# Gated MLP with split weights: low parts two at a time from a ring of five places, token sums in another rhythm, two early down passes, returns in pieces

## The chip, the cores and the metric

The kernel runs on one core of a Trainium2 chip. Its time is the device time of the program in microseconds (us); the median of several runs counts, and lower is better.

The core's engines work side by side and meet through semaphores: TensorE (PE) multiplies matrices, VectorE (DVE) and ScalarE (ACT) do elementwise work, GpSimd (POOL) has little to do here, and SyncE (SP) issues the DMA transfers. Each engine takes its instructions in the order in which the program lists them.

## The reference, cut to what matters

A decoder trunk of two layers on 256 tokens of width 2048, all in float32. Layer 0 mixes tokens by a block sparse attention (MoBA), layer 1 by a latent attention (MLA), and both are followed by a gated MLP of inner width 5632:

```python
def conv_glu_ffn(h, w_gate, w_up, conv_w, conv_b, w_down):
    g = h @ w_gate
    g = lax.conv_general_dilated(g, conv_w[:, None, :], ..., feature_group_count=g.shape[-1]) + conv_b
    return (jax.nn.silu(g) * (h @ w_up)) @ w_down

for i in range(DEPTH):                       # DEPTH = 2
    h = rms_norm(x, attn_norm[i])
    x = x + mixer(h)                         # MoBA, then MLA
    h = rms_norm(x, ffn_norm[i])
    x = x + conv_glu_ffn(h, ffn_w_gate[i], ffn_w_up[i], ffn_conv_w[i], ffn_conv_b[i], ffn_w_down[i])
```

The change is in the MLPs and in how weights are split for them.

## The kernel before, in words

**Split weights.** Weights come from HBM as float32 in units of 128x1024 (`raw`, 512 KB, six units ahead); a unit is two pieces of 512 columns. TensorE works with rounded numbers, so each piece is split: ACT casts it to a high part (`whi`, line 183), DVE subtracts that from the piece, which gives the low part (`wlo`, line 184). The tokens are split likewise. TensorE then makes three products of a piece: high by high, high by low tokens, low by high tokens (lines 402 to 404, twelve matmuls of 128x256 for a plain piece). The low part is read by the third matmul of a piece first, at line 404.

**The order.** The program is a list of quanta, one per piece, and TensorE goes through them. `ws.split(q + 4)` is called at quantum q, so a piece is split four pieces ahead; `at(q, f)` hangs other work of ACT, DVE and SP on a quantum. High and low parts come from two pools of five tiles, so piece i takes the place of piece i - 5.

**The MLP.** Its 600 pieces a layer are 432 plain ones (gate, up and down projections) and 168 block products. For six groups of four tiles of 128 inner columns, the gate projection is made by a scheme with fewer products: seven products in place of eight, from sums of weights and sums of tokens. A group is 28 products (4 quarters `kq` of the width, seven products each), each six matmuls (lines 1181 to 1183). Three products of a quarter read weights as loaded (`xroom`), four read sums of weights that DVE makes (`weight_sum`, line 1159). Products stand between plain pieces, one or two plain ones for each, by `BLOCK_EVERY`. The matmuls of a group end in transposed form; `mixed` and `cross` (lines 1198 on) add them up in `a_mix`, 14 quanta later DVE's stream transposes (line 516) write the result into `xroom`, four transfers carry it to DRAM (`there<-xroom`), one brings it back. The sum for the next group overwrites the room of the transposes.

**The token sums.** At the start of an MLP, for each quarter, ACT scales four tiles of tokens (`tokens`, line 1072) into `done`, a part of `a_mix`; DVE makes four sums (`token_sum`, line 1088), and these are split in two halves (`token_high`, line 1097; `token_low`, line 1101, 128x512 each). Quarters follow each other at 8 quanta.

**Room.** The tokens `xT` go to DRAM during the MLP (`kept`), and their room holds block weights, weight sums and transposes (`xroom`). Early on, one down pass multiplies the first 16 tiles of inner columns (`DOWN_FIRST` = 4 quarters), so that their room (`a_one`) can be used again; its 16 partial results per layer go to DRAM through ACT copies (`keep_down`, line 1108, `part<-y`, two `y` buffers). Behind the last group, `load_down` fetches them in one transfer (`a_back<-part`, 2048 KB), `leave_room` fetches `xT` in four, two quanta apart, and DVE scales and adds them (`down_scaled`, line 1118, and `down_added`).

Behind that, a pass of plain down pieces ends the layer.

Of the kernel before, what the change touches and what calls it, by code (L numbers as in the profile page):

```python
# [17 lines left out]
P = 128  # L18
S = 256
# [24 lines left out]
AHEAD_PIECES = 4  # L44

# [3 lines left out]
ROOM = 64  # L49
# [13 lines left out]
A_ONE, A_TWO = 4 * DOWN_FIRST, 12  # L63
# [24 lines left out]
class Inner:  # L88


    def __init__(self, pool):
        self.pool, self.tiles = pool, {}
        written = [j for kind, *what in gate_up_order() if kind == "plain" for j in what[:1] if what[1:] == [1, 3]]
        later = [j for j in written if j >= A_ONE]
        homes = ("one", range(A_ONE)), ("two", later[:A_TWO]), ("three", later[A_TWO:])
        self.home = {j: (name, i) for name, js in homes for i, j in enumerate(js)}
        self.size = {name: len(js) for name, js in homes}
        assert self.size["three"] <= A_ONE
        for name in ("one", "two"):
            self.tile(name)  # L100
# [4 lines left out]
    def tile(self, name):  # L105
        if name not in self.tiles:
            n, tag = (A_ONE, "a_one") if name != "two" else (self.size[name], None)
            self.tiles[name] = self.words(name, n, F32R, tag).rearrange("p (j s) -> p j s", s=2 * S)
        return self.tiles[name]
# [7 lines left out]
class Stream:  # L117
# [3 lines left out]
    def __init__(self, nc, raw_pool, part_pool, units, starts, pieces):  # L121
        self.starts = starts
# [4 lines left out]
        self.loaded = self.split_to = 0  # L127

# [35 lines left out]
    def split(self, upto):  # L164
        while self.split_to < min(upto, len(self.pieces)):
            i = self.split_to
            u, j, n = self.pieces[i]
            if u is None:
                b, c = BY_BLOCK
                w = j()  # L170
            else:
                self.load(u + AHEAD_UNITS)
                w = self.raw[u][:, j * n : (j + 1) * n]
                b, c = self.starts(u, j)
            hi = self.part_pool.tile([P, 512 + ROOM], F32R, name="whi")[:, b : b + max(n, 512)]
            lo = self.part_pool.tile([P, 512 + ROOM], F32R, name="wlo")[:, c : c + max(n, 512)]
            hi_, lo_ = hi[:, :n], lo[:, :n]
            if len(w.shape) == 4:
                hi_, lo_ = (x.rearrange("p (i j f) -> p i j f", i=2, j=2) for x in (hi_, lo_))
            if i == 0:  # L180
                self.nc.vector.tensor_copy(hi_, w)
            else:
                self.nc.scalar.copy(hi_, w)  # L183
            self.nc.vector.tensor_tensor(lo_, w, hi_.bitcast(F32), op=ALU.subtract)  # L184
            self.parts[i] = (hi, lo, n)
            self.split_to += 1
            for f, args in self.after.pop(i, ()):
                f(*args)

# [5 lines left out]
def trunk(ctx: ExitStack, tc: tile.TileContext, a, out):  # L195
# [4 lines left out]
    part_pool = ctx.enter_context(tc.tile_pool(name="parts", bufs=AHEAD_PIECES + 1))  # L200
# [25 lines left out]
    block_pieces = {}  # L226

    def gate_up_units(layer):
# [12 lines left out]
        for kind, *what in tokens:  # L241
            if kind == "block":
                block_pieces[(layer, *what)] = len(pieces)
                pieces.append((None, lambda layer=layer, what=what: blocks[layer].source(*what), 512))
            elif kind == "down":
                if at_ % 2 == 0:
# [6 lines left out]
                    downs_unit = len(units) - 1  # L253
                pieces.append((downs_unit, at_ % 2, 512))
                at_ += 1
            else:
                j, up, kq = what
                if kq % 2 == 0:
                    units.append(per[(2 * j + up) * 2 + kq // 2])
                    plain_unit = len(units) - 1  # L260
                pieces.append((plain_unit, kq % 2, 512))
        return pieces

# [24 lines left out]
    ws = Stream(nc, raw_pool, part_pool, units, starts, pieces_of(units))  # L288
# [764 lines left out]
    class Blocks:  # L1053
# [7 lines left out]
        def open(self):  # L1061
# [4 lines left out]
            self.done = mix[:, : 4 * S]  # L1066
# [13 lines left out]
        def token_sum(self, step):  # L1080
            y = self.done.rearrange("p (i e t s) -> p e t i s", i=2, e=2, t=NT)
            a11, a12, a21, a22 = y[:, 0, 0], y[:, 1, 0], y[:, 0, 1], y[:, 1, 1]
            x0, x1 = (self.mix[:, 4 + i].rearrange("p (i s) -> p i s", i=2) for i in range(2))
            out, x, y, op = (
                (x0, a21, a22, ALU.subtract), (x1, a11, a21, ALU.subtract),
                (x1, x0, a11, ALU.subtract), (x0, x1, a12, ALU.add),
# [3 lines left out]
        def token_parts(self, kq, c):  # L1090
            src = self.mix[:, 4:6].rearrange("p c (i s) -> p c i s", i=2)
            hi, lo = (self.parts[:, c : c + 2, 2 * kq : 2 * kq + 2, h] for h in range(2))
            return src, hi, lo

        def token_high(self, kq, c):
            src, hi, _ = self.token_parts(kq, c)
            nc.scalar.copy(hi, src)

        def token_low(self, kq, c):
            src, hi, lo = self.token_parts(kq, c)  # L1100
# [3 lines left out]
        def keep_down(self, state, j):  # L1104
            if j == 0:
                self.part = dram.tile([P, KD, S], F32, name="part")
            y = ffn["pool"].tile([P, S], F32, name="y")
            nc.scalar.copy(y, state["acc"][:, :S])
            nc.sync.dma_start(self.part[:, j], y)

        def load_down(self):
            self.back = ffn["a"].words("back", 8, F32, "a_sums").rearrange("p (j s) -> p j s", s=S)
            nc.sync.dma_start(self.back, self.part)
# [10 lines left out]
        def take_room(self):  # L1124
            room = keep.tile([P, KD * S], F32, name="xroom", tag="xT")
            self.rawq = [room[:, i * 1024 : (i + 1) * 1024] for i in range(2)]
            self.wsum = [room[:, (4 + i) * 512 : (5 + i) * 512] for i in range(4)]
            self.turn = room[:, 6 * 512 :]
# [18 lines left out]
        def total(self, i):  # L1147
            return self.wsum[i].rearrange("p (i j f) -> p i j f", i=2, j=2)

# [128 lines left out]
    def plan_gate(f, q, behind):  # L1278
# [3 lines left out]
        f.ready = behind(q, 9)  # L1282
# [8 lines left out]
    def plan_ffn(layer, norm, next_norm):  # L1291
# [17 lines left out]
        for kind, *what in tokens:  # L1309
# [12 lines left out]
            if kind == "down":  # L1322
                j, kq = what
                opens = kq in (0, DOWN_FIRST)
# [3 lines left out]
                end = (DOWN_FIRST if kq < DOWN_FIRST else NF // 4) - 1  # L1328
                q = add(lambda t_hi, t_lo, n, st=st, kq=kq, opens=opens, end=end: feat_major(
                    st, lambda: ffn["a"], 4 * kq, 4 * end + 3, opens, t_hi, t_lo, n))  # L1330
                if kq == DOWN_FIRST and j == 0:
                    q_down = q
                if kq == DOWN_FIRST - 1:
                    at(behind(q, 2), block.keep_down, st, j)
# [386 lines left out]
    ws.split(1)  # L1721
    for f, args in side.pop(-1):
        f(*args)
    for q, (f, args) in enumerate(quanta):
        for g, gargs in ahead.pop(q, []):
            g(*gargs)
        ws.split(q + min(1 + q // 6, AHEAD_PIECES))
# [10 lines left out]
def gate_up_order():  # L1738

    def full(j):  # L1740
        return [("plain", j, up, kq) for up in range(2) for kq in range(4)]

    def up(j):
        return [("plain", j, 1, kq) for kq in range(4)]
# [4 lines left out]
    def down(j):  # L1749
        return [("down", j, kq) for kq in range(DOWN_FIRST)]  # L1750

    inside = [j for js in BLOCK_GROUPS for j in js]
    fulls = [j for j in range(NF) if j not in inside]
    downs, missing = list(range(KD)), set(range(A_ONE))
    waiting, order, now = [], [], []
    n, ups, most, ready = 0, 0, 2, None

    def plain(k):
        nonlocal now, n, ups, ready
        for _ in range(k):  # L1760
            if not now:
                begun = ready is not None and ready <= n and downs
                if not (waiting or fulls or begun):
                    return
                if waiting and (not (fulls or begun) or (waiting[0][0] <= n and ups < most)):
                    now, ups = up(waiting.pop(0)[1]), ups + 1
                elif begun:
                    now, ups = down(downs.pop(0)), 0
                else:
                    now, ups = full(fulls.pop(0)), 0  # L1770
            order.append(now.pop(0))
            n += 1
            if order[-1][0] == "plain" and order[-1][2:] == (1, 3) and order[-1][1] in missing:
                missing.remove(order[-1][1])
                if not missing:
                    ready = n + DOWN_WAIT

    plain(BLOCK_LEAD)
    for g, js in enumerate(BLOCK_GROUPS):
        for i, one in enumerate(group(g)):  # L1780
            order.append(one)
            plain(BLOCK_EVERY[i % len(BLOCK_EVERY)])
        waiting += [(n + BLOCK_BACK, j) for j in js]
        most = 2 if g + 1 < len(BLOCK_GROUPS) else 4
        plain(BLOCK_GAP)
    plain(8 * NF)
    assert not (downs or fulls or waiting)
    return order + [("down", j, kq) for j in range(KD) for kq in range(DOWN_FIRST, NF // 4)]
# [109 lines left out]
```

## Time and profile before

| | |
|---|---|
| median of 3 runs | 2047.77 us (2047.41 to 2047.81) |
| profiled execution | 2048.13 us, of which the span of the profile is 2045.9 us |
| granted TensorE clock | 1.00 |
| busy share: PE, PEld, DVE, ACT, POOL | 100%, 96%, 81%, 63%, 2% |
| HBM read, written | 411.16 MB, 26.35 MB (214 GB/s) |
| mixed part of the MLP, layer 0 and layer 1 | 382 to 880 us, 1341 to 1840 us |
| last down pass, layer 0 and layer 1 | 880 to 1085 us, 1841 to 2040 us |

How the rows of the profile are read: a group of instructions has its line, engine, operation, output <- inputs by their names in the program, the shape and the count; then, behind a bar, busy us in all and mean ns of one; then the idle time of the engine right before them, with what ended most of it. `L184 DVE ... wlo<-raw,whi` are the low parts of plain pieces, `wlo<-xroom,whi` those of block products. In a timeline a row is start us, duration us, engine, line, operation; idle time before it stands in brackets. In the chain of waits a row is start, duration, engine, tile and line, and a chain runs back from the last instruction over what released each step.

### The profile page before, as it was taken

The page shows a single profiled execution, that of the slowest core. Times are in us where ns is not written, and L with a number is a line of the kernel's source. Part 1 is how long each engine was busy: PE and PEld are TensorE (multiplying, and loading weights), DVE is VectorE, ACT ScalarE, POOL GpSimd, SP SyncE. Part 2 cuts the span into 40 slices and gives each one's busy share as a digit, 9 for nine tenths or more (in the row PEclk, how much of TensorE's full clock was granted, in tenths as well). Part 3 has the DMA queues.
Part 4 walks back from the last instruction along what each step waited for, and adds up shares of the span by engine and source line. Part 5 has one row for each costly group of instructions (what it writes and reads, how often), then busy time and mean ns, then how long its engine had stood idle before and what let it go on. Part 6 is the DMA issues. An engine that isn't in the chain of part 4 may idle for free.

```text
span 2045.9 us, 43563 instructions
## 1 busy us (share of the span) xinstructions
PE 2037.8 (100%) x16300; PEld 1970.4 (96%) x16300; DVE 1660.1 (81%) x3211; ACT 1290.9 (63%) x2474; POOL 48.7 (2%) x38
## 2 busy tenths in 40 slices
PE   9999999999999999999999999999999999999999
PEld 7888899999999999999999889999999999999999
DVE  7877777788998888888666998778889888898655
ACT  6656666666666666655556786666666666666443
POOL 0010000000000000000000110000000000000000
PEclk9999999999999999999999999999999999999999
DMA  7777776676766776676655646567666767758664
GB/s 274 235 250 223 226 231 210 211 233 203 225 218 207 237 239 189 223 267 208 199 196 159 210 152 183 189 214 234 207 214 217 227 217 227 225 186 301 202 211 129
DMA packets 162531, 440.35 MB, mean 215 GB/s; under 512 B 18816, under 2 KB 42880, under 8 KB 162064
## 3 DMA queue, kind: packets, MB, share of 16 engines
q1 hardware_dynamic: 162000, 437.21, 66.6%
q8 instruction: 127, 2.08, 0.4%
q14 instruction: 84, 0.69, 0.1%
q10 hardware_dynamic: 288, 0.33, 0.1%
q0 software_dynamic: 32, 0.04, 0.0%
HBM read 411.16 MB, written 26.35 MB: 214 GB/s over the span
## 4 chain that ended last, share of the span: by engine, by line
PE 97%; DVE 2%; ACT 0%; DMA 0%; issue 0%; SPq 0%; DVEq 0%; ACTq 0%
PE acc L404 23%; PE acc L403 22%; PE acc L402 22%; PE acc L376 16%; PE tp L1183 2%; PE tp L1181 2%; PE tp L1182 2%; PE sc L1183 2%; PE sc L1182 2%; PE sc L1181 2%; DVE wlo L184 1%; PE sc L657 0%; PE sc L656 0%; PE sc L655 0%; PE sc L758 0%; DMA xT<-in_xT 0%
## 5 line engine op out<-in xcount | busy, mean ns | idle before, releaser
L183 ACT CAST whi<-raw 128x512 fp32r<-128x512 f32 (+1 forms) x1271 | 775.6, 621 | 437.4 <-PE acc L403 223.4
L184 DVE TENSOR_TENSOR wlo<-raw,whi 128x512 fp32r<-128x512 f32 (+1 forms) x1272 | 861.1, 689 | 199.0 <-ACT whi L183 170.2
L404 PE MATMUL acc<-h,wlo 128*128 128x256 f32 x2112 | 585.3, 277 | 0.5 <-DVE wlo L184 0.5
L402 PE MATMUL acc<-h,whi 128*128 128x256 f32 x2112 | 585.1, 277 | 0.0
L403 PE MATMUL acc<-h,whi 128*128 128x256 f32 x2112 | 585.0, 277 | 0.0
L404 PEld LDWEIGHTS acc<-h,wlo 128*128 128x128 f32 x2112 | 396.5, 188 | 1.5 <-DVE wlo L184 1.4
L403 PEld LDWEIGHTS acc<-h,whi 128*128 128x128 f32 x2112 | 396.5, 188 | 0.0
L402 PEld LDWEIGHTS acc<-h,whi 128*128 128x128 f32 x2112 | 396.5, 188 | 0.0
L183 ACT CAST whi<-xroom 128x512 fp32r<-128x512 f32 x336 | 208.9, 622 | 102.6 <-PE acc L403 76.6
L376 PE MATMUL acc<-whi,h 128*128 128x512 f32 (+1 forms) x896 | 265.7, 377 | 0.9 <-ACT h L424 0.9
L184 DVE TENSOR_TENSOR wlo<-xroom,whi 128x512 fp32r<-128x512 f32 x336 | 231.1, 688 | 18.9 <-ACT whi L183 9.2
L376 PEld LDWEIGHTS acc<-whi,h 128*128 128x128 f32 x896 | 164.8, 188 | 31.1 <-ACT h L424 1.4
L376 PE MATMUL acc<-wlo,h 128*128 128x512 f32 (+1 forms) x448 | 168.8, 377 | 0.3 <-DVE wlo L184 0.2
L402 PE MATMUL acc<-oT,whi 128*128 128x256 f32 x512 | 142.8, 279 | 0.0
L403 PE MATMUL acc<-a_one,whi 128*128 128x256 f32 x512 | 142.0, 277 | 0.0
L404 PE MATMUL acc<-a_one,wlo 128*128 128x256 f32 x512 | 142.0, 277 | 0.0
L402 PE MATMUL acc<-a_one,whi 128*128 128x256 f32 x512 | 141.9, 277 | 0.0
L404 PE MATMUL acc<-oT,wlo 128*128 128x256 f32 x512 | 141.9, 277 | 0.0
L403 PE MATMUL acc<-oT,whi 128*128 128x256 f32 x512 | 141.8, 277 | 0.0
L402 PE MATMUL acc<-a_three,whi 128*128 128x256 f32 x512 | 141.3, 276 | 0.0
L403 PE MATMUL acc<-a_three,whi 128*128 128x256 f32 x512 | 141.3, 276 | 0.0
L404 PE MATMUL acc<-a_three,wlo 128*128 128x256 f32 x512 | 141.3, 276 | 0.0
(256 smaller groups left out, 3997.8 us busy)
## 6 DMA issues: line engine op xcount, KB each, us to landing
raw<-in_ffn_gu SPq DMA_DIRECT2D x256, 512.0 KB, 4.8
raw<-in_ffn_down SPq DMA_DIRECT2D x144, 512.0 KB, 4.8
xroom<-in_ffn_gu SPq DMA_DIRECT2D x192, 256.0 KB, 4.6
raw<-in_moba_wk SPq DMA_DIRECT2D x32, 512.0 KB, 5.8
raw<-in_moba_wv SPq DMA_DIRECT2D x32, 512.0 KB, 5.0
raw<-in_moba_wo SPq DMA_DIRECT2D x32, 512.0 KB, 4.8
raw<-in_ffn_down SPq DMA_DIRECT2D x64, 256.0 KB, 4.3
raw<-in_mla_wo SPq DMA_DIRECT2D x32, 512.0 KB, 3.8
```

The costliest lines, as they stand in the source:

```text
L183: self.nc.scalar.copy(hi_, w)
L184: self.nc.vector.tensor_tensor(lo_, w, hi_.bitcast(F32), op=ALU.subtract)
L376: mm(state["acc"][t][:, :n], src[:, kt, c : c + P], (t_lo if part == 1 else t_hi)[:, :n], start=kt == 0 and part == 0, stop=kt == k_last a ...
L402: mm(o, w_hi, src[:, kt, :S], start=first and k == 0, stop=False, skip_group_check=True)
L403: mm(o, w_hi, src[:, kt, S:], start=False, stop=False, skip_group_check=True)
L404: mm(o, w_lo, src[:, kt, :S], start=False, stop=kt == k_last, skip_group_check=True)
L1181: mm(o, x[:, 0], w_hi, start=opens and i == 0, stop=False, skip_group_check=True)
L1182: mm(o, x[:, 1], w_hi, start=False, stop=False, skip_group_check=True)
L1183: mm(o, x[:, 0], w_lo, start=False, stop=last and i == 1, skip_group_check=True)
```

## The change

- **Ring.** `whi` and `wlo` become one tile each with five places (`SLOTS`), and a piece takes the place that was used longest ago. In the MLPs, two pieces get one subtraction of 128x2x512 for both low parts, if the ring has two places: the two pieces of a unit, and the weight sums of products 3 and 4, and of 5 and 6. The casts stay one per piece. As built, 432 pairs are so joined and 728 low parts of 512 stay single.
- **Token sums.** Four tokens come within two quanta, the four sums within two, and one `token_high` and one `token_low` take all 1024 columns. `done` is a tile of its own.
- **Down passes.** Two early passes (quarters 0 and 1, quarters 2 and 3) stand in place of one, so 32 partial results a layer go out, in two arrays. The first group has tiles 8 to 11, and groups have 36 plain pieces each.
- **Returns.** `xT<-kept` and `a_back<-part` are asked for in four steps, ten quanta apart, `a_back` in pieces of 512 KB; DVE adds the two partial results (`down_summed`).

```diff
@@ Stream
+        self.high, self.low = (
+            part_pool.tile([P, SLOTS * SLOT], F32R, name=name).rearrange("p (k c) -> p k c", c=SLOT)
+            for name in ("whi", "wlo")
+        )
...
+    def split_these(self, i, now):
...
+        mate, both = self.mates.get(i, (None, None))
+        if mate is not None:
+            held = sum(k >= now for k in self.last_use)
+            wanted = sum(k != mate and k not in self.parts for k in range(i + 1, now + AHEAD_PIECES))
+            if held + 2 + wanted > SLOTS:
+                mate = None
+        these = [i] if mate is None else [i, mate]
+        slots = sorted(sorted(range(SLOTS), key=lambda k: self.last_use[k])[: len(these)])
...
+            two = slice(slots[0], slots[1] + 1, slots[1] - slots[0])
+            hi, lo, src = self.high[:, two, b : b + n], self.low[:, two, c : c + n], both()
+        self.nc.vector.tensor_tensor(lo, src, hi.bitcast(F32), op=ALU.subtract)
@@ constants
-BLOCK_EVERY = 2, 1, 1, 1, 2, 1, 1
-BLOCK_GROUPS = tuple(tuple(range(4 * g, 4 * g + 4)) for g in (0, 6, 7, 8, 9, 10))
-DOWN_FIRST, DOWN_WAIT = 4, 6
+BLOCK_PLAIN = (36,) * 6
+BLOCK_GROUPS = tuple(tuple(range(4 * g, 4 * g + 4)) for g in (2, 6, 7, 8, 9, 10))
+DOWN_PASSES, DOWN_WAIT = (2, 4, NF // 4), 6
@@ plan_ffn
             for k in range(4):
-                at(q + k, block.tokens, 4 * kq + k)
-            at(q + 3, block.keep_tokens, kq)
-            for step in range(2):
-                for half in range(2):
-                    at(q + 4 + 3 * step + half, block.token_sum, 2 * step + half)
-                at(q + 6 + 3 * step, block.token_high, kq, 2 * step)
-                at(q + 7 + 3 * step, block.token_low, kq, 2 * step)
+                at(q + k // 2, block.tokens, 4 * kq + k)
+                at(q + 3 + k // 2, block.token_sum, k)
+            at(q + 2, block.keep_tokens, kq)
+            at(q + 6, block.token_high, kq)
+            at(q + 8, block.token_low, kq)
...
         q = last_block + 9
-        at(q, block.load_down)
         for kq in range(4):
-            at(q + 1 + 2 * kq, block.leave_room, kq)
-        for j in range(0, KD, 2):
-            at(q_down - 12 + 2 * j, block.down_scaled, j)
-            at(q_down - 10 + 2 * j, block.down_added, j)
+            at(q + 1 + 10 * kq, block.leave_room, kq)
+            at(q + 5 + 10 * kq, block.load_down, kq)
+            for j in (4 * kq, 4 * kq + 2):
+                k = q + 17 + 10 * kq + 2 * (j % 4)
+                at(k, block.down_summed, j)
+                at(k + 1, block.down_scaled, j)
+                at(k + 2, block.down_added, j)
```

Three places show what stands in a row on an engine (line, operation, output <- inputs, shape; the lines of the changed program are others: 229 is the low part, 569 the transposes, 1226 the weight sum, 1141 and 1154 the token sums and their low parts). First DVE behind the fifth group of layer 0, before:

```order
L1159 TENSOR_TENSOR xroom<-xroom 128x512
L516 STREAM_TRANSPOSE xroom<-a_mix 128x4x4x32 x2
L184 TENSOR_TENSOR wlo<-raw,whi 128x512
L184 TENSOR_TENSOR wlo<-xroom,whi 128x512
L1159 TENSOR_TENSOR xroom<-xroom 128x512
L1269 TENSOR_TENSOR c<-c,acc 128x256
L184 TENSOR_TENSOR wlo<-raw,whi 128x512
L184 TENSOR_TENSOR wlo<-xroom,whi 128x512
L1159 TENSOR_TENSOR xroom<-xroom 128x512
L184 TENSOR_TENSOR wlo<-raw,whi 128x512
```

and now:

```order
L569 STREAM_TRANSPOSE xroom<-a_mix 128x4x4x32 x2
L1328 SCALAR_TENSOR_TENSOR c<-g,par,c 128x256 x2
L1226 TENSOR_TENSOR xroom<-xroom 128x512
L1343 TENSOR_TENSOR a_again_8983<-c,a_again_8983 128x256
L229 TENSOR_TENSOR wlo<-xroom,whi 128x512
L1226 TENSOR_TENSOR xroom<-xroom 128x512
L229 TENSOR_TENSOR wlo<-raw,whi 128x2x512
L1336 TENSOR_TENSOR c<-c,acc 128x256
L229 TENSOR_TENSOR wlo<-xroom,whi 128x512
L1226 TENSOR_TENSOR xroom<-xroom 128x512 x2
L229 TENSOR_TENSOR wlo<-xroom,whi 128x2x512
```

A quarter has four weight sums; the third and the fourth write the room that the transposes used. Before, the third is the last line 1159 here, with the low part of a plain piece right behind it. Now the third and the fourth stand together (`x2`), the plain piece's low part is part of a pair further up, and the low parts of products 3 and 4 follow as a pair.

Then DVE where the token sums of a quarter are made, before:

```order
L1088 TENSOR_TENSOR a_mix<-a_mix 128x256
L184 TENSOR_TENSOR wlo<-raw,whi 128x512
L1269 TENSOR_TENSOR c<-c,acc 128x256
L1088 TENSOR_TENSOR a_mix<-a_mix 128x256
L184 TENSOR_TENSOR wlo<-raw,whi 128x512 x2
L1248 TENSOR_TENSOR g<-acc,rstd_b 128x256
L1101 TENSOR_TENSOR a_sums<-a_mix,a_sums 128x2x2x128
L1088 TENSOR_TENSOR a_mix<-a_mix 128x256
L184 TENSOR_TENSOR wlo<-raw,whi 128x512
L1276 TENSOR_TENSOR a_one<-c,a_one 128x256
L1088 TENSOR_TENSOR a_mix<-a_mix 128x256
L184 TENSOR_TENSOR wlo<-raw,whi 128x512 x2
```

and now:

```order
L1141 TENSOR_TENSOR a_mix<-done 128x256 x2
L1141 TENSOR_TENSOR a_mix<-a_mix,done 128x256 x2
L229 TENSOR_TENSOR wlo<-raw,whi 128x2x512
L1336 TENSOR_TENSOR c<-c,acc 128x256
L229 TENSOR_TENSOR wlo<-raw,whi 128x2x512
L1315 TENSOR_TENSOR g<-acc,rstd_b 128x256
L1343 TENSOR_TENSOR a_down_3966<-c,a_down_3966 128x256
L1154 TENSOR_TENSOR a_sums<-a_mix,a_sums 128x4x2x128
L229 TENSOR_TENSOR wlo<-raw,whi 128x2x512
L1328 SCALAR_TENSOR_TENSOR c<-g,par,c 128x256 x2
L229 TENSOR_TENSOR wlo<-raw,whi 128x2x512
```

The four sums stand together, and one low part of 128x4x2x128 follows.

Then SP behind the last group of layer 0, before:

```order
L1113 DMA a_back<-part 128x4096
L141 DMA raw<-in_ffn_gu 128x1024
L1134 DMA xT<-kept 128x1024
L141 DMA raw<-in_ffn_gu 128x1024
L1134 DMA xT<-kept 128x1024
L141 DMA raw<-in_ffn_gu 128x1024
L1134 DMA xT<-kept 128x1024
L141 DMA raw<-in_ffn_gu 128x1024
L1134 DMA xT<-kept 128x1024
```

and now:

```order
L578 DMA done<-there_10300 128x1024
L158 DMA raw<-in_ffn_gu 128x1024
L1198 DMA xT<-kept 128x1024
L158 DMA raw<-in_ffn_gu 128x1024 x2
L1171 DMA a_back<-part 128x1024 x2
L158 DMA raw<-in_ffn_gu 128x1024 x3
L1198 DMA xT<-kept 128x1024
L158 DMA raw<-in_ffn_gu 128x1024 x2
L1171 DMA a_back<-part 128x1024 x2
L158 DMA raw<-in_ffn_down 128x1024 x3
L1198 DMA xT<-kept 128x1024
L154 DMA raw<-in_ffn_down 128x512 x2
```

The returns, which stood alternately with one unit of weights each, lie between two or three units each, and the partial results come in two pieces per step.

More of the change, by code (lines that the diff above doesn't have):

```diff
@@ L162, in begin, with raw_of, split @@
         self.loaded = AHEAD_UNITS
-    def split(self, upto):
+    def raw_of(self, i):
+        u, j, n = self.pieces[i]
+        if u is None:
+            return j()
+        self.load(u + AHEAD_UNITS)
+        return self.raw[u][:, j * n : (j + 1) * n]
+    def split(self, upto, now):
         while self.split_to < min(upto, len(self.pieces)):
             i = self.split_to
[L167 to L185, printed above, removed]
+            if i not in self.parts:
+                self.split_these(i, now)
             self.split_to += 1
@@ L1281, in plan_gate @@
         at(behind(q, 5), f.conv_rest)
-        f.ready = behind(q, 9)
+        f.ready = behind(q, 10)
         at(f.ready, f.silu)
@@ L1323, in plan_ffn @@
                 j, kq = what
-                opens = kq in (0, DOWN_FIRST)
+                number = next(i for i, k in enumerate(DOWN_PASSES) if kq < k)
+                opens, end = kq in (0, *DOWN_PASSES), DOWN_PASSES[number] - 1
                 if opens:
@@ L1327, in plan_ffn @@
                 st = out_states[j]
[L1328 removed]
                 q = add(lambda t_hi, t_lo, n, st=st, kq=kq, opens=opens, end=end: feat_major(
                     st, lambda: ffn["a"], 4 * kq, 4 * end + 3, opens, t_hi, t_lo, n))
[L1331 to L1334, printed above, removed]
+                if kq == end and end + 1 < NF // 4:
+                    at(behind(q, 2), block.keep_down, st, j, number)
                 elif kq == end:
@@ L1738, in gate_up_order, with plain @@
 def gate_up_order():
[L1740 to L1744, printed above, removed]
+    def plain(j, up):
+        return [("plain", j, up, kq) for kq in range(4)]
     def group(g):
         return [("block", g, kq, s) for kq in range(4) for s in range(7)]
-    def down(j):
-        return [("down", j, kq) for kq in range(DOWN_FIRST)]
     inside = [j for js in BLOCK_GROUPS for j in js]
-    fulls = [j for j in range(NF) if j not in inside]
@@ L1754, in gate_up_order @@
-    downs, missing = list(range(KD)), set(range(A_ONE))
+    fulls = [plain(j, 0) + plain(j, 1) for j in range(NF) if j not in inside]
+    downs, missing, ready = [], [], []
+    for a, b in zip((0, *DOWN_PASSES), DOWN_PASSES[:-1]):
+        downs.append([[("down", j, kq) for kq in range(a, b)] for j in range(KD)])
+        missing.append(set(range(4 * a, 4 * b)))
     waiting, order, now = [], [], []
-    n, ups, most, ready = 0, 0, 2, None
-    def plain(k):
-        nonlocal now, n, ups, ready
+    n, ups, most = 0, 0, 2
@@ L1771, in plain @@
             order.append(now.pop(0))
             n += 1
[L1773 to L1778, printed above, removed]
+            if order[-1][0] == "plain" and order[-1][2:] == (1, 3):
+                for m in missing:
+                    m.discard(order[-1][1])
+                while len(ready) < len(missing) and not missing[len(ready)]:
+                    ready.append(n + DOWN_WAIT)
@@ L1781, in gate_up_order @@
             order.append(one)
-            plain(BLOCK_EVERY[i % len(BLOCK_EVERY)])
+            m = BLOCK_PLAIN[g]
+            fill((i + 1) * m // 28 - i * m // 28)
+        before = len(waiting)
         waiting += [(n + BLOCK_BACK, j) for j in js]
[L1784 to L1788, printed above, removed]
+        most = 8 if g + 1 < len(BLOCK_GROUPS) else 16
+        fill(BLOCK_GAP)
+        assert len(waiting) <= 4 or not before
+    fill(8 * NF)
+    assert not (any(downs) or fulls or waiting)
+    return order + [("down", j, kq) for j in range(KD) for kq in range(DOWN_PASSES[-2], NF // 4)]
 def wo_order(opened):
```

147 lines of the change are left out of this document (104 added, 43 removed).

## The prediction

> **What bounds the kernel now.** I read the page's engine line and the chain of waits first, then the busy times by stage, then the chain's rows, then DVE's groups and timeline.
>
> ```profile
> span 2045.9 us, 43563 instructions
> PE 2037.8 (100%) x16300; PEld 1970.4 (96%) x16300; DVE 1660.1 (81%) x3211; ACT 1290.9 (63%) x2474; POOL 48.7 (2%) x38
> PE 97%; DVE 2%; ACT 0%; DMA 0%; issue 0%; SPq 0%; DVEq 0%; ACTq 0%
> ```
>
> TensorE sets the end: busy all along, and 97% of the chain. The change leaves its instructions and their shapes alone, so it can only move the gaps between matmuls. How large these are, the busy time of stretches tells (start:end, length, then busy us and instructions of PE, PEld, DVE, ACT, POOL; clock; DMA share; GB/s):
>
> ```profile
> 382.00:880.00 498.00, 497.50 (x4354) 496.88 (x4353) 436.45 (x780) 330.01 (x604) 0.00 (x0) 1.00 0.68 218
> 1341.00:1840.00 499.00, 499.00 (x4364) 498.30 (x4363) 436.94 (x781) 329.61 (x605) 0.00 (x0) 1.00 0.69 218
> 880.00:1085.00 205.00, 205.00 (x1811) 205.00 (x1810) 147.92 (x271) 111.60 (x205) 0.00 (x0) 1.00 0.66 220
> ```
>
> The first two hold the mixed part of the two MLPs (block products among plain pieces), the third a pass of plain down pieces alone. The third gives the floor, 205.00 / 1811 = 0.1132 us a matmul. At that pace 4354 and 4364 matmuls take 492.9 and 494.0 us; the mixed parts lie 5.1 and 5.0 us above. **About 10 us is all that any reordering of the MLPs could win.** DVE is 436.45 / 498.00 = 88% busy there, the fullest engine behind PE.
>
> What of the 10 us is DVE's shows in the chain of waits, which breaks its PE runs where a matmul waited (start, duration, engine and tile; an undisturbed step is 0.11):
>
> ```profile
> 423.28 0.34 PE acc L404
> 819.89 0.68 DVE wlo L184
> 820.62 0.39 PE acc L404
> 822.27 0.28 PE sc L1183
> 823.14 0.34 PE acc L404
> ...
> 1382.28 0.35 PE acc L404
> 1499.02 0.38 PE acc L404
> 1553.41 0.31 PE acc L404
> 1555.00 0.25 PE sc L1183
> 1781.91 0.32 PE acc L404
> ```
>
> All of these matmuls read the low part. Seven of them take 0.23 + 0.17 + 0.23 + 0.24 + 0.27 + 0.20 + 0.21 us over 0.11, that at 1555.00 another 0.14, and that at 820.62 starts 0.68 late and runs 0.11 longer by PE's timeline:
>
> ```profile
> 819.83 0.28 PE L403 MATMUL acc<-h,whi 128*128 128x256 f32 x1
> 820.62 0.39 PE L404 MATMUL acc<-h,wlo 128*128 128x256 f32 x1 [0.51 <-DVE wlo L184]
> ```
>
> Together 0.79 + 1.55 + 0.14 = **2.5 us wait for a low part**. The other 7 us or so of the excess I ascribe to the 168 changes from a block product to a plain piece in each layer (7 / 336 = 0.02 us each); their number stays.
>
> **The change part by part.**
>
> *Pairs.* The groups of instructions (mean ns of one behind the comma) and one stretch of DVE give the prices:
>
> ```profile
> L184 DVE TENSOR_TENSOR wlo<-raw,whi 128x512 fp32r<-128x512 f32 x1256 | 849.2, 688 | 198.6 <-ACT whi L183 169.8 <-PE tp L1182 9.7 <-PE sc L1182 8.8
> L1088 DVE TENSOR_TENSOR a_mix<-a_mix 128x256 f32<-128x256 f32 x32 | 13.5, 422 | 0.3
> ...
> 816.19 0.69 DVE L184 TENSOR_TENSOR wlo<-raw,whi 128x512 fp32r<-128x512 f32 x1
> 816.79 0.69 DVE L184 TENSOR_TENSOR wlo<-xroom,whi 128x512 fp32r<-128x512 f32 x1
> 819.27 0.69 DVE L1159 TENSOR_TENSOR xroom<-xroom 128x512 f32<-128x512 f32 x1 [1.79 <-DMA there<-xroom]
> 819.88 0.68 DVE L184 TENSOR_TENSOR wlo<-raw,whi 128x512 fp32r<-128x512 f32 x1
> ```
>
> 432 operations of 1024 columns take the place of 864 of 512. 256 columns take 0.422 and 512 take 0.688, so 1024 should take 0.688 + 2 x 0.266 = 1.22 (estimate; no such operation is in the trace). Busy time falls by 864 x 0.688 - 432 x 1.22 = 67 us, but operations in a row start 0.60 apart (816.19, 816.79), so the engine is really freed of 2 x 0.60 - (1.22 - 0.09) = 0.07 a pair, **about 30 us of its 1660**. It was not the bound, so that buys nothing by itself; at most it removes the 2.5 us. The Trainium skill, "VectorE: DVE Perf Modes", section "The DRAIN you can't avoid", says that a next operation starts only when the pipe is empty, but that one which is not held starts earlier. By the first the saving would be 67 us, by the second 30; the 0.60 agrees with the second, and TensorE's sum is the same by both.
>
> Against it stands a delay: the low part of the first piece of a pair now waits for both casts and for 1024 columns. The steps from a free place to TensorE, by the chain at the start of the kernel, PE's and ACT's timelines at 818 us:
>
> ```profile
> 10.45 0.52 ACT whi L183
> 11.00 0.70 DVE wlo L184
> 11.74 36.81 PE acc L376 x161
> ...
> 818.81 0.28 PE L403 MATMUL acc<-h,whi 128*128 128x256 f32 x1
> 819.12 0.62 ACT L183 CAST whi<-xroom 128x512 fp32r<-128x512 f32 x1 [0.70 <-PE acc L403]
> 422.41 1.13 ACT L183 CAST whi<-raw 128x512 fp32r<-128x512 f32 x2
> ```
>
> The last high matmul of a place to the cast 0.31; cast to DVE 0.55; DVE to matmul 0.74, so 0.74 + 1.22 - 0.69 = 1.27 for 1024 columns. Two casts in a row cost 1.13 - 0.62 = 0.52 more. So the pair needs 0.31 + 0.52 + 0.55 + 1.27 = **2.65 us** from the release of its second place; one operation of 512 would need 0.31 + 0.55 + 0.74 = 1.60. A ring of five, with the fourth and fifth taken as a pair, leaves in the worst order three pieces between: product, plain, product, 0.68 + 1.36 + 0.68 = 2.72, plus 0.45 until the first low matmul: 3.17 (6 and 12 matmuls at 0.1132 a piece). The spare is **0.52 us for 20 pairs a layer, 1.04 for 16 more**, and over 1.2 for the other 180. Today a piece takes the place of the fifth before it, four pieces between: 4.08 + 0.45 - 1.60 = 2.93 of spare at least. With one DVE operation ahead (0.60) the 0.52 is about used up, with two 0.7 is lost. Lower bound: no place loses. Upper: a third of the 40 tightest, since DVE waited for ACT in only 39 of some 600 low parts of the first mixed part:
>
> ```profile
> DVE wlo L184 <- ACT whi L183: 23.5, 39, 1.2
> ```
>
> Otherwise there was work in front; but not where the pairs are, because DVE has 30 us more rest. I take a tenth: 40 x 0.1 x 0.7 = **+2.8 us**.
>
> *Sums of groups.* Of the 2.5 us, 0.79 + 0.17 + 0.23 = 1.2 stand behind DVE's 1.79 us wait at 819.27 for the transfer of the transposes: there the third weight sum waits, and a plain piece's low part (819.88) stood behind it and was late. Now that low part and product 2's are in front, and behind the transfer come the third sum, the fourth and the pair of products 3 and 4: 0.60 + 0.60 + 1.27 = 2.47 until product 3's matmul. Before, product 2's, due a product and a plain piece earlier, took the sum, the plain low part, the fourth sum, one of 256 columns and a single, 3 x 0.60 + 0.33 + 0.74 = 2.87. So most of the 1.2 should go too; a gain of 1.3 without it is the lower bound, and I take 2.5.
>
> *Token sums.*
>
> ```profile
> 417.38 0.52 ACT L1072 ACTIVATE a_mix<-xT,par 128x256 f32<-128x256 f32 x1 [1.32 <-DVE a_mix L1088]
> L1097 ACT CAST a_sums<-a_mix 128x512 fp32r<-128x512 f32 x16 | 9.9, 619 | 16.3 <-DVE a_mix L1088 16.3
> ```
>
> The 0.23 at 423 comes of this: ACT waited 1.32 for the buffer, and its casts came late. The separate tile takes that wait away. In exchange four token activations and two casts come in two plain pieces: 4 x 0.41 + 2 x 0.52 = 2.68 (each 0.52 and 0.62 long, less the 0.1 by which two in a row overlap) against 2.72, so ACT has nothing to spare there for eight places; I take 0, and at most 8 x 0.23 = 1.8, if each comes out as the place at 423 did. Four operations of 256 in a row on DVE (4 x 0.33 = 1.3) delay a low part by less than the slack of a run of plain pieces.
>
> *Second early down pass and returns.*
>
> ```profile
> L1108 ACT COPY y<-acc 128x256 f32<-128x256 f32 x32 | 11.8, 370 | 12.1 <-PE acc L404 12.1
> L1118 DVE TENSOR_TENSOR a_back<-a_back,rstd_b 128x512 f32<-128x512 f32 x16 | 11.0, 686 | 0.0
> part<-y SPq DMA_DIRECT2D x32, 128.0 KB, 3.9
> a_back<-part SPq DMA_DIRECT2D x2, 2048.0 KB, 11.4
> ```
>
> 32 more copies on ACT (32 x 0.37 = 12 us in 1000, at 63% busy), 16 more adds on DVE (16 x 0.686 = 11 us of the 30 saved), 32 more small writes and 14 more reads on SP's queue. Two y buffers are handed out every two plain pieces, so a buffer has 2 x 2 x 1.36 = 5.4 us, and a write lands in 3.9. A return is used 12 quanta (16 us) after it is asked for, where 2048 KB took 11.4 and now 512 KB go. Hidden, 0; uncovered it would be 5.4 - 3.9 = 1.5 us short, for a few of 64 places.
>
> *Spacing of groups and of the first group's tiles*: 36 plain pieces a group, evenly; count and switches stay: 0.
>
> Sum: -2.5 + 2.8 = **+0.3 us**. The profiled execution took 2048.13 (span 2045.9 and 2.2 around it), 0.36 above the median 2047.77; on the median's basis this is 2048.1, and since a tenth may be high I set **2047.9**. What a measurement here tells from no change is 0.2%, 4.1 us.
>
> **The rivals.**
>
> *C, the gain alone.* The freed DVE has no place late; everything of the 2.5 goes: 2045.3. For it: 30 us of rest; against: the 1.2 behind the transfer, which still lands late. Still within 0.2%.
>
> *B, the ring is too tight (slower).* Its place is the pair taken at the fourth and fifth place in front of a product, its price 0.7 each, and it decides where DVE is two operations behind. A third of the 40 tightest: 13.3 x 0.7 = 9.3, less 2.5: +6.8, 2054.6. For it: 1.04 and 0.52 of spare against 2.9, and the queue in order, as the 1.79 us wait shows, behind which a ready low part (819.88) stood. The Trainium skill, "Perfetto Trace Analysis", section "Tensor Engine Instruction (MATMUL, LD_WEIGHTS)", calls the queues of ACT and DVE strict FIFO; the trace agrees, and the price by it is the same. Against it: with the waits that the changed order carries and the durations above, five such places, worked through, come out 0.2 to 0.55 early.
>
> *F, the switches become cheaper.* If part of the 7 us was DVE's after all, up to 2.5 + 2 = 4.5 goes: 2043.3. Against it: those gaps show no DVE in the chain.
>
> *D, the strided pair holds the ring.* If an operation on places 1 and 4 is waited for as if it touched 2 and 3, each pair holds PE for about 0.7: 432 x 0.7 = 300 us, 2350. Against it: the waits built into the changed program name single places.
>
> **How the numbers follow.** A 0.58, C 0.20, B (with the y buffers and ACT's crowding) 0.17, F 0.03, D 0.02. The forecast is A, 2047.9; its own range is 2045.8 (a gain of 2.5, and a fiftieth of the 40 late: 0.6) to 2050 (a gain of 1.3, and an eighth late: 3.5). The range reaches C and B: 2045.2 to 2055.0. Faster than 2043.7 is F alone, 0.03; slower than 2051.9 is B and D, 0.19; the rest 0.78.
>
> **What will show it.** Pairs right: 432 operations of 128x1024 at 1.22, and DVE's busy time near 1660 - 67 + 16 x 0.686 - 1 (eight token low parts for sixteen) = 1603. Delay wrong: more rows of L404's or the products' successor in the chain than nine, above all in front of products. Token sums right: no wait of ACT for a_mix. Returns right: no wait for a_back or xT. The forecast fails if the two mixed parts change by over 4 us together, or if anything outside them moves, since nothing is changed there.

## The result

The changed kernel took **2059.19 us** (median of 4 runs, 2056.03 to 2061.35), the kernel before 2047.79 (2047.41 to 2047.88): a ratio of **1.0055** with a 95% interval of 1.0037 to 1.0072. It is 11.4 us slower, where 2047.9 was forecast in a range up to 2055.0. Its runs also lie 5 us apart, those of before 0.5 (2 to 3 us where 23 or 24 runs of it were taken later). Runs in which a lower TensorE clock was granted (0.75 in one of 2538.6 us) stand in none of the numbers here.

The profiled execution of the change was its fastest, 2056.03 us, 7.9 more than that of before. The engine line and the chain of waits of its page:

```profile
span 2053.8 us, 42716 instructions
PE 2038.8 (99%) x16300; PEld 1970.9 (96%) x16300; DVE 1632.7 (80%) x2787; ACT 1276.3 (62%) x2498; POOL 48.8 (2%) x38
PE 89%; issue 6%; DVE 2%; DMA 2%; ACT 1%; POOL 0%; SPq 0%; POOLq 0%; ACTq 0%; DVEq 0%
```

DMA is now in the chain. That TensorE's part of it fell from 97% to 89% is for the most part not lost time: at the start of the second MLP TensorE waits for POOL, and from there the chain runs back over POOL, which had nothing to do for 102.88 us ("issue", below). What was lost is read from the mixed parts of the two MLPs, in the same stretches as before:

```profile
382.00:880.00 498.00, 495.47 (x4330) 494.38 (x4328) 421.74 (x632) 325.99 (x612) 0.00 (x0) 1.00 0.69 221
1341.00:1840.00 499.00, 494.56 (x4319) 493.22 (x4318) 421.32 (x632) 325.04 (x611) 1.71 (x1) 1.00 0.69 221
```

24 and 45 matmuls fewer got through, at 0.1132 us each 2.7 and 5.1 us: nearly all of the 7.9. The rows of the chain show one stall of each of three kinds:

```profile
669.34 0.43 SPq L1204
669.87 7.13 DMA part<-y
677.86 0.63 ACT whi L219
678.52 1.24 DVE wlo L229
679.80 0.39 PE acc L457
...
818.86 1.23 DVE wlo L229
820.13 0.39 PE acc L457
...
1240.06 102.88 issue
1342.94 1.75 POOLq L1961
1344.74 0.43 PE tp L534 x2
```

**First kind: ACT stands at a y copy.** ACT's timeline at 671 us, with the copy of 667.11:

```profile
667.11 0.36 ACT L1161 COPY y<-acc 128x256 f32<-128x256 f32 x1
...
671.23 0.36 ACT L1161 COPY y<-acc 128x256 f32<-128x256 f32 x1
671.56 0.62 ACT L219 CAST whi<-xroom 128x512 fp32r<-128x512 f32 x1
672.92 0.62 ACT L219 CAST whi<-xroom 128x512 fp32r<-128x512 f32 x1 [0.74 <-PE acc L456]
677.07 0.37 ACT L1161 COPY y<-acc 128x256 f32<-128x256 f32 x1 [3.54 <-DMA part<-y]
677.34 1.14 ACT L219 CAST whi<-raw 128x512 fp32r<-128x512 f32 x2
```

DVE's, a little later, and SP's:

```profile
678.52 1.22 DVE L229 TENSOR_TENSOR wlo<-raw,whi 128x1024 fp32r<-128x1024 f32 x1 [4.25 <-ACT whi L219]
```

```profile
667.87 1.90 SPq L1204 DMA_DIRECT2D xroom<-in_ffn_gu  x4
669.87 0.38 SPq L1162 DMA_DIRECT2D part<-y  x1
```

The copy of 677.07 waits for the buffer that the copy of 667.11 filled. SP issued that one's write at 669.87 only, behind four loads of block weights, and it landed 7.13 us later. Two casts and their pair stand behind the copy, and TensorE waits. Stalls with this wait stand at 527, 678, 1489 and 1642 us and cost 0.63 + 2.04 + 1.55 + 1.35 = 5.6 us. (At 527 the profile names a matmul as what ended ACT's wait of 2.12 us; but the write of that buffer landed at 524.24, and the copy began at 524.31.)

**Second kind: a pair behind other work on DVE** (780, 820, 1557, 1744, 1783 us; 3.0 us together).

**Third kind: TensorE waits for the norm's `rstd`**, which POOL makes, at the start of both MLPs. Before, it had no idle time there:

```profile
381.80 0.43 PE L534 MATMUL tp<-ident,rstd 128*128 128x128 f32 x2 [0.63 <-POOL rstd L528]
1344.74 0.43 PE L534 MATMUL tp<-ident,rstd 128*128 128x128 f32 x2 [1.14 <-POOL rstd L528]
```

5.6 + 3.0 + 1.8, less the 2.5 us of old stalls, which are gone or replaced, is 7.9.

### The profile page after: what moved, and what is told of

Same layout as the page of the kernel before. It is cut to its first block, busy times and chain, and to the rows that moved or that the text cites. A ratio compares the mean times of both kernels' runs of the same rounds, so it can differ in the third digit from the quotient of the medians.

```text
span 2053.8 us, 42716 instructions
## 1 busy us (share of the span) xinstructions
PE 2038.8 (99%) x16300; PEld 1970.9 (96%) x16300; DVE 1632.7 (80%) x2787; ACT 1276.3 (62%) x2498; POOL 48.8 (2%) x38
## 4 chain that ended last, share of the span: by engine, by line
PE 89%; issue 6%; DVE 2%; DMA 2%; ACT 1%; POOL 0%; SPq 0%; POOLq 0%; ACTq 0%; DVEq 0%
PE acc L457 20%; PE acc L455 20%; PE acc L456 20%; PE acc L429 15%; PE tp L1250 2%; PE tp L1249 2%; PE tp L1248 2%; PE sc L1250 2%; PE sc L1249 2%; PE sc L1248 2%; DVE wlo L229 1%; ACT whi L219 1%; DMA part<-y 0%; DMA raw<-in_ffn_gu 0%; DMA raw<-in_mla_wqn 0%
## 5 line engine op out<-in xcount | busy, mean ns | idle before, releaser
L219 ACT CAST whi<-raw 128x512 fp32r<-128x512 f32 (+1 forms) x1271 | 749.7, 620 | 492.9 <-PE acc L456 306.0
L229 DVE TENSOR_TENSOR wlo<-raw,whi 128x512 fp32r<-128x512 f32 (+2 forms) x888 | 806.8, 919 | 304.0 <-ACT whi L219 291.2
L229 DVE TENSOR_TENSOR wlo<-xroom,whi 128x512 fp32r<-128x512 f32 (+1 forms) x288 | 223.1, 775 | 18.3 <-ACT whi L219 17.1
L457 PE MATMUL acc<-a_down,wlo 128*128 128x256 f32 x512 | 142.2, 278 | 4.0 <-DVE wlo L229 4.0
L455 PE MATMUL acc<-a_down,whi 128*128 128x256 f32 x512 | 141.9, 277 | 0.2 <-ACT whi L219 0.2
L456 PE MATMUL acc<-a_down,whi 128*128 128x256 f32 x512 | 141.9, 277 | 0.0
L455 PE MATMUL acc<-a_again,whi 128*128 128x256 f32 x512 | 141.3, 276 | 0.0
L456 PE MATMUL acc<-a_again,whi 128*128 128x256 f32 x512 | 141.3, 276 | 0.0
L457 PE MATMUL acc<-a_again,wlo 128*128 128x256 f32 x512 | 141.3, 276 | 0.0
```

The costliest lines, as they stand in the source:

```text
L219: self.nc.scalar.copy(hi_, src)
L229: self.nc.vector.tensor_tensor(lo, src, hi.bitcast(F32), op=ALU.subtract)
L455: mm(o, w_hi, src[:, kt, :S], start=first and k == 0, stop=False, skip_group_check=True)
L456: mm(o, w_hi, src[:, kt, S:], start=False, stop=False, skip_group_check=True)
L457: mm(o, w_lo, src[:, kt, :S], start=False, stop=kt == k_last, skip_group_check=True)
```

## The experiments

The two theories behind the first experiments: **Y**, the y buffers stop ACT; **P**, the ring is too tight for pairs.

**More y buffers.** The copies take turns between the two `y` buffers and the norm's three `nsq` buffers.

```diff
-            y = ffn["pool"].tile([P, S], F32, name="y")
+            if j % 2:
+                y = ffn["pool"].tile([P, S], F32, name="y")
+            else:
+                y = small.tile([P, S], F32, name="nsq", bufs=3)
```

> The changed kernel, with the y copies of the early down passes taken in turn from the two y buffers and from the three nsq buffers of the norm (idle at that time), so that a buffer is asked for again after four or six copies and not after two. Theory Y (ACT stands at a y copy until the write of the copy before the last has landed, and the casts of the next pieces stand behind it): the four stalls with such a wait in the profile of the change, 0.63 + 2.04 + 1.55 + 1.35 = 5.6 us, go and the runs come together: 2050 to 2052, all within 1 us of each other. Rival P (the ring of five is too tight for pairs, the y wait only shows up where pairs are late anyway): 2055 to 2061 as before, with the same spread.

Measured 2050.66 (2050.35 to 2051.37), ratio to before 1.0013 (1.0004 to 1.0022). 8.5 us are gone and the runs lie 1 us apart: with pairs in place, the y wait is the larger part of the loss, and the spread goes with it. It is not all.

**The same without pairs.**

```diff
-    ws = Stream(nc, raw_pool, part_pool, units, starts, pieces_of(units), mates)
+    ws = Stream(nc, raw_pool, part_pool, units, starts, pieces_of(units), {})
```

> As the kernel with more y buffers, and in addition every piece gets a low part of its own, as before the change (ring of five, same order of pieces, 864 operations of 512 in place of 432 of 1024). Theory Y: what is left after the y buffers is small, so this is within 2 us of the kernel with pairs and more y buffers: 2048 to 2051. Rival P: this one alone comes back to 2047 to 2048.5 while the one with pairs stays at 2055 or more. If pairs help at all here, this is slower than the one with pairs.

Measured **2045.88** (2045.31 to 2046.12), ratio 0.9987 (0.9978 to 0.9997): faster than before, and 4.8 faster than with pairs. Its mixed parts:

```profile
382.00:880.00 498.00, 498.00 (x4366) 498.00 (x4366) 438.20 (x777) 334.88 (x619) 0.00 (x0) 1.00 0.69 222
1341.00:1840.00 499.00, 499.00 (x4375) 499.00 (x4375) 439.88 (x781) 335.56 (x620) 0.00 (x0) 1.00 0.69 223
```

TensorE has no gap of over 0.1 us left there. (498 + 499) - (4366 + 4375) x 0.1132 = 7.5 us stay over the floor: about the 7 us that the prediction ascribed to the changes from product to plain piece. The trace bears this out: behind such a change (some 170 in the first stretch) the first three matmuls start 118, 122 and 118 ns apart where others take 113 to 114, 0.018 us a change and 3.1 us in this stretch.

**Without pairs, with two y buffers** (the second edit alone).

> The changed kernel without pairs (two y buffers as in the change). Theory Y: ACT stands at the y copies as long as with pairs (3 to 3.5 us at a time), but a single low part is ready 1.05 us sooner than that of a pair, so each such stall shrinks by up to 1 us: 2051 to 2057, still with a spread of some us. Rival P: 2047 to 2049 and no spread.

Measured 2045.88 (2045.35 to 2047.34), ratio 0.9989 (0.9979 to 0.9999). ACT waits for the writes as long as in the change, but it comes to its copies earlier, so that it waits more often for TensorE's result instead. The waits (us in all, times, longest) of this kernel:

```profile
ACT y L1161 <- PE acc L457: 16.5, 20, 1.4
ACT y L1161 <- DMA part<-y: 11.3, 8, 3.1
```

and of the change:

```profile
ACT y L1161 <- DMA part<-y: 11.7, 5, 3.5
ACT y L1161 <- PE acc L457: 6.3, 8, 1.2
```

So both theories had a half. The y wait alone costs 0.5 us in this kernel's profile and nothing in the median, pairs alone 4.8, both together 13.3 (2059.19 - 2045.88; the kernel before, measured beside each, moved from 2047.79 to 2048.17, so such differences are good to some 0.4 us).

**Ring and pairs alone, in the kernel before.**

> The kernel before with the ring and the pairs alone: order of pieces, token sums, down pass and returns as before. There a y buffer has four plain pieces and products between two copies, twice the time. Theory Y: no y stall, so 2046 to 2050 with the spread of the kernel before (0.5 us). Rival P: 9 to 12 us of stalls from the ring, 2054 to 2060.

Measured 2064.7 to 2068.3 in three runs, ratio 1.0086 (1.0070 to 1.0103): worse than the change. The same kernel ran once more, for its profile:

> The kernel before with ring and pairs alone once more, for a profile (the one taken was at a granted clock of 0.75). Theory T: 45 tight pairs a layer, and the stalls stand at low parts of such pairs, about 17 us more than before in the two mixed parts and nothing outside but the wait for rstd (1.4 us). The other theory (the order of the kernel before, with its token sums, makes ACT late): stalls at the token sums at the start of the MLPs, above all.

2068.12, above what Y and P gave. The largest part stands where this expectation's other theory put it, at the token sums. The chain of waits in the first MLP:

```profile
405.57 1.15 ACT whi L208 x2
406.74 1.23 DVE wlo L218
408.30 0.61 DVE a_sums L1143
410.32 0.63 ACT whi L208
410.97 1.24 DVE wlo L218
```

and ACT's timeline there:

```profile
405.05 0.62 ACT L1139 CAST a_sums<-a_mix 128x512 fp32r<-128x512 f32 x1 [1.96 <-DVE a_mix L1130]
409.39 0.51 ACT L1114 ACTIVATE a_mix<-xT,par 128x256 f32<-128x256 f32 x1 [2.38 <-DVE a_mix L1130]
```

Stalls of 0.3 to 1.3 us recur every 12 us from 399 to 436 and from 1370 to 1406, where token sums are made, 7.1 us in all. There ACT and DVE wait for each other in turn: ACT's cast for a sum that stands behind a pair on DVE, the pair for casts behind ACT's wait. The rest is at the `rstd`, at group ends, and some 3 us at 897 and 920 us, behind the mixed part.

**The old token rhythm under pairs**, in the changed kernel with five y buffers. The functions for the sums go back too; the schedule is shown:

```diff
-                at(q + k // 2, block.tokens, 4 * kq + k)
-                at(q + 3 + k // 2, block.token_sum, k)
-            at(q + 6, block.token_high, kq)
-            at(q + 8, block.token_low, kq)
+                at(q + k, block.tokens, 4 * kq + k)
+            for step in range(2):
+                for half in range(2):
+                    at(q + 4 + 3 * step + half, block.token_sum, 2 * step + half)
+                at(q + 6 + 3 * step, block.token_high, kq, 2 * step)
+                at(q + 7 + 3 * step, block.token_low, kq, 2 * step)
```

> The changed kernel with five y buffers (2050.7), but with the token sums in the rhythm of the kernel before (one sum per quantum, two high and two low parts of 512 a quarter). With ring and pairs alone, put into the kernel before, the profile has four stalls of 0.4 to 1.4 us a layer where the token sums are made, 7.1 us in all. If it is the old rhythm under pairs that makes them, they come back: 2056 to 2059. If it was something else in the order of the kernel before, 2050 to 2052.

Measured 2059.97 (2059.19 to 2061.33): 9.3 more than with the new rhythm, a little over the expectation, and the four stalls a layer are back. With pairs, the respaced sums are needed at the start of an MLP.

**Which pairs?** By the order of the program, every stall of the first two kinds in the change stands at a pair whose second place is released with product, plain, product (2.72 us) in between. First such pairs were given up, then all others.

```diff
+        if mate is not None:
+            p = max(sorted(self.last_use)[:2])
+            between = sum(1 if self.pieces[k][0] is None else 2 for k in range(p + 1, i))
+            if between < 5:        # the other kernel: between > 4
+                mate = None
```

> The changed kernel (two y buffers), but a pair is given up where only product, plain, product (2.72 us) lie between the last use of its second place and its first piece: 360 pairs stay, all with a plain piece more in between (3.4 us or more). In the profile of the change the stalls at 527, 680, 780, 820, 1491, 1557, 1644, 1744 and 1784 us all stand at pairs of the tight kind, the four with a y wait too. Theory T (the loss is at the tight pairs, and the y wait costs only what they have not got): 2046 to 2049, of which up to 1.4 for the wait for rstd at the start of the second MLP, with a spread under 1.5. Rival S (any pair takes the slack that covers the y wait): 2053 to 2060 with some us of spread.

Measured 2053.77 (2050.16 to 2055.82): theory T falls, and the time lies in rival S's range. With two y buffers, 360 pairs with more room lose 7.9 against none, and ACT stands 16.5 us at the writes.

> The reverse: pairs only where product, plain, product or less lie between; all other pieces have a low part of their own. 120 pairs (refusing the others shifts the ring, so there are more tight ones than the 72 of the change). Theory T: it keeps the loss, 2056 or more, with some us of spread. Rival S: 120 pairs of 432 keep about a quarter of the 13 us between the change and the kernel without pairs, 2047 to 2050.

Measured 2050.07 (2048.66 to 2051.85): 120 tight pairs lose 4.2 us. That is 0.035 us a pair, against 7.9 / 360 = 0.022 of the others: tight ones cost more, but the others are not free while the buffers are short. (These 120 are not the 72 tight pairs of the change: other pieces then take other places.)

**Early places, or the long operation?** Pairs are taken as they were, casts too, but with two operations of 512.

```diff
+        for k, src in zip(these, w):
+            hi, lo, n = self.parts[k]
...
+            self.nc.vector.tensor_tensor(lo, src, hi.bitcast(F32), op=ALU.subtract)
```

> The changed kernel with its 432 pairs taken as they are (two places at once, the two casts in a row, in the same order on ACT), but with two operations of 512 columns where it has one of 1024. Theory M (what is late is the first piece's low part, which waits for the second place, the second cast and 1024 columns): 2046 to 2048. Rival R (the second cast, taken early, waits for a place on ACT and holds everything behind it): the loss stays, 2053 to 2060.

Measured 2050.09 (2048.64 to 2051.66), between the two expectations. 4.2 of the 13.3 us come with the early casts on ACT alone (2050.09 - 2045.88), 9.1 with joining the low parts.

**The write's place in SP's queue.**

```diff
-            nc.sync.dma_start(self.part[number][:, j], y)
+            nc.scalar.dma_start(self.part[number][:, j], y)
```

> The changed kernel (432 pairs, two y buffers), with the writes of the partial results issued by ACT itself, right behind its copy, and not by SP. In the profile of the change the copy of 667.11 was issued by SP at 669.87 only, behind four loads of block weights, and landed 7.1 us later. If the place in SP's queue makes the y wait, a buffer comes back 2 to 5 us sooner and the four stalls of 5.6 us go to 1 or less: 2050 to 2053, with a spread under 2. If the landing itself is late whoever issues it (the engines are shared with the weights), it stays: 2055 to 2061.

Measured 2051.48 (2050.59 to 2053.26): 7.7 less than the change, with its two y buffers. The writes of this kernel among the DMA issues (the last number is the median us from issue to landing), and its wait:

```profile
part<-y ACTq DMA_DIRECT2D x64, 128.0 KB, 3.9
```

```profile
ACT y L1161 <- DMA part<-y: 3.3, 5, 1.0
```

The writes of the change:

```profile
part<-y SPq DMA_DIRECT2D x64, 128.0 KB, 3.7
```

The landing is no faster, and the wait falls from 11.7 to 3.3 us: what is gone is the time in front of the issue, in SP's order. Its runs still lie 2.7 us apart, where under 2 was expected. The Trainium skill, "DMA: Bandwidth & Descriptors", section "Issuing engines are not separate DMA queues", says that issuing from another engine saves only the initiating sequencer's time, usually small beside the DMA itself. The first half agrees (3.9 against 3.7). Here the time in front of the issue was not small (2.4 us of the write of 667.11, against 7.13 behind), since four loads stood in front.

**The start of the MLP.** Five y buffers, and no pairs in the first 16 pieces.

```diff
-                    mates[first_piece] = len(pieces), lambda u=plain_unit: whole(u)
+                    if j > 1:
+                        mates[first_piece] = len(pieces), lambda u=plain_unit: whole(u)
```

> The changed kernel with five y buffers (2050.7), without pairs in the first 16 pieces of each MLP; 416 stay. In the kernels with pairs the rstd operation on POOL at the start of each MLP takes 1.72 us and not 1.09, while DVE works on 1024 columns beside it, and at the second MLP TensorE waits 1.4 us for it. If the pair beside it is the cause: POOL's operation back at 1.09 us, and 1.2 to 1.5 us less, 2049.1 to 2049.6. If not: 2050.3 to 2051.

Measured 2048.99 (2048.53 to 2049.48), 1.7 less, and POOL's operation is back at 1.09 us. The expectation of 1.2 to 1.5 less counted the wait of the second MLP alone; that of the first goes too. The group in this kernel:

```profile
L529 POOL TENSOR_TENSOR rstd<-ms,mhalf 128x2 f32<-128x2 f32 x4 | 4.4, 1089 | 964.7 <-DVE ms L527 964.7
```

and in the change, where two of the four stand beside pairs:

```profile
L528 POOL TENSOR_TENSOR rstd<-ms,mhalf 128x2 f32<-128x2 f32 x4 | 5.6, 1400 | 967.7 <-DVE ms L526 967.7
```

**All three cures** (the last edit, five y buffers, tight pairs given up).

> All three cures at once: five y buffers, no pairs in the first 16 pieces of an MLP, and no pair where only product, plain, product lie between; 344 pairs stay. If what pairs cost is these three things (the y wait, rstd, the tight places), it is as fast as the kernel without pairs: 2045.4 to 2046.6. If every pair costs something by itself, 344 of 432 keep some 80% of what is left (4.8 less 1.4): 2048 to 2049.5.

Measured 2048.34 (2047.95 to 2048.93), ratio 1.0003 (0.9993 to 1.0012): at the lower end of the second expectation. 344 pairs still cost 2.5 us against none. In its profile the stalls over 0.1 us sum to 2.1 us, most of the 2.5; the largest are at products at the start of the last group (820.40 and 1779.30).

The 13.3 us, taken away in this order: 8.5 with the y buffers, 1.7 with `rstd`, 0.65 with the tight places, 2.5 with the remaining pairs. In another order the terms are others: without pairs the y buffers are worth nothing. The last two terms are near the spread of the runs. Why the remaining pairs stall at those products was not tested.

## Why the prediction was wrong

- **The gain was right, but not by the freed DVE.** 2.5 us of old stalls were said to go at most. Without pairs the change is 2045.88 against 2048.17 measured beside it, 2.3 less, and the stalls are gone, though DVE is busy for 1669.6 us there (with five y buffers), more than the 1660.1 of before. So the rest of the change won it, its ring and the order of the other work, and case C's 2045.3 is nearly met for another reason than C's. Which part removed which stall was not tested.
- **The step that failed is that two terms were priced apart: "40 x 0.1 x 0.7 = +2.8" for the pairs and "Hidden, 0" for the writes.** Both together cost 13.3. The mechanism of the first was named (spare of 0.52 us, two operations ahead on DVE), and rival B had its place and sign. What the pair lost to DVE's work alone, the second kind, is 3.0 us in the profile, near the 2.8; that is in part luck, since I counted 20 pairs a layer at 0.52 and 16 at 1.04, while all 36 have only product, plain, product in between. Left out was ACT: its waits of 3 us, which single low parts absorb (0.5 us lost), fall on the same slack, of which a pair leaves too little for them.
- **"Hidden, 0" for the second down pass holds without pairs and fails with them.** A buffer was said to have 5.4 us and a write to land in 3.9. 3.9 is the median from the issue. The trace of before had the row that speaks against it, for its 32 writes (line 1109):

```profile
DMA to landing us min/median/max: 1.7/3.9/8.0
```

  In the change, the write of 667.11 was issued 2.4 us after its copy had ended and landed after 7.13, 9.5 against 5.4. Neither the maximum nor SP's order in front of the issue was in my sum, and the price, "1.5 us short, for a few of 64 places", left out that casts queue behind the copy. Measured, with pairs: 8.5 us.
- **"Nothing is changed" outside the mixed parts failed at their edge.** Pairs begin with the first pieces of the MLP, next to `rstd`: 1.7 us that no term held.
- **Price of the pair right, DVE's total misread.** The operation takes what was estimated, 1.22:

```profile
L229 DVE TENSOR_TENSOR wlo<-raw,whi 128x1024 fp32r<-128x1024 f32 x384 | 469.6, 1223 | 240.2 <-ACT whi L219 231.9 <-DMA raw<-in_ffn_gu 3.8 <-PE sc L1250 3.6
L229 DVE TENSOR_TENSOR wlo<-xroom,whi 128x1024 fp32r<-128x1024 f32 x48 | 58.6, 1222 | 11.6 <-ACT whi L219 11.2
```

  The 1603 for DVE's busy time came from durations; the page has 1632.7. 1669.6 without pairs less 1632.6 with them (both with five y buffers) is 37 us, near the 30 by starts.
- **Token sums, returns:** the 0 held, and the stall at 423 went. That the old rhythm would cost 9.3 us under pairs was not seen. **D** and **F** did not occur.
- **"Sums of groups" did not hold under pairs.** The stalls at 820 and 1783 (0.95 each) are of the size of the old 820 stall (0.79), but from another cause: behind a pair and the transposes stands DVE's step for the convolution (line 1328), for which ACT waits with casts behind it:

```profile
816.83 0.42 ACT L1333 ACTIVATE c<-c 128x256 f32<-128x256 f32 x1 [2.48 <-DVE c L1328]
817.15 1.13 ACT L219 CAST whi<-raw 128x512 fp32r<-128x512 f32 x2
```

## What to carry to other kernels

Joining two operations of an engine that is not the bound bought no time here and spent slack twice: the first result waits for the second input, and whatever queues behind the longer operation waits too. Before slack is spent, find every other wait that lives on it, by the maximum of a transfer's time from the copy that feeds it, issue delay in SP's order included, and not by the median of its landing. Do not add up the costs of two changes that live on the same slack. When runs of a changed kernel spread by microseconds where the old one's did not, look for a buffer whose return hangs on a transfer.

## What the runs showed of the hardware

A GpSimd operation on 128x2 values is held up by a VectorE operation beside it. POOL's and DVE's timelines at the start of the second MLP, before:

```profile
1339.64 1.09 POOL L475 TENSOR_TENSOR rstd<-ms,mhalf 128x2 f32<-128x2 f32 x1 [102.31 <-DVE ms L473]
```

```profile
1339.48 0.69 DVE L184 TENSOR_TENSOR wlo<-raw,whi 128x512 fp32r<-128x512 f32 x1
```

and in the change:

```profile
1342.98 1.71 POOL L528 TENSOR_TENSOR rstd<-ms,mhalf 128x2 f32<-128x2 f32 x1 [102.92 <-DVE ms L526]
```

```profile
1342.91 1.23 DVE L229 TENSOR_TENSOR wlo<-raw,whi 128x1024 fp32r<-128x1024 f32 x1
```

In both it ends some 0.55 us after the DVE operation (1340.73 after 1340.17, 1344.69 after 1344.14), so 0.54 more on DVE became 0.62 more on POOL, and TensorE waited. Without pairs at the start of the MLP it was 1.09 us again. The Trainium skill, "SBUF — State Buffer", section "Who interferes with whom", says that a DVE instruction with two SBUF inputs contends with a GpSimd instruction that reads SBUF, because its second input comes through the shared read interface. The rows agree, and it was not weighed in the prediction.
